# The second projection of a gated feed-forward layer as seven half-size products

## The chip, the cores and the metric

One of the cores of a Trainium2 chip runs the kernel. TensorE (PE) does the matrix products into PSUM, VectorE (DVE), ScalarE (ACT) and GpSimd (POOL) do the element-wise work, and SyncE (SP) issues all transfers between SBUF and DRAM. The metric is the time of one execution in device microseconds (us), the median of several runs.

## The reference, cut to what matters

One decoder layer on 16 learned tokens and 1024 tokens of width 1024: a mixer (a state-space group beside an attention group, then an output projection), and a feed-forward layer of width D_FF = 2816. The change is in the last two lines of the feed-forward layer:

```
gu = xn @ w_up                                   # first projection: 1024 -> 2 * 2816
g = causal_dwconv(gu[..., :D_FF], ffn_conv_w, ffn_conv_b)
f = (gelu(g) * gu[..., D_FF:]) @ w_down          # second projection: 2816 -> 1024
h = h + rms_norm(f, ffn_post_g)
return h[:, N_META:]
```

All data are float32. Each operand of a large product is split into a rounded part and the rest (hi and lo), and three of the four partial products are summed, so a block of 128 features costs three matmul instructions.

## The kernel before, in words

The first projection (class `Problem`, lines 963 to 1097) is already done in seven half-size products. A problem is one pair of 128-feature blocks of either the gate half (`g`, gu = 0) or the other half (`u`, gu = 1); there are 22 problems, g0, u0, g1, u1 to g10, u10. `product(n)` does one of the seven products (order 1, 6, 5, 7, 2, 3, 4) into PSUM banks called A, X and Y, and `post(n)` has DVE and ACT add the banks up. For g, `scale` (ACT) and `taps` (two DVE instructions) do the convolution and `gelu` (ACT) follows. For u, `after_u` multiplies the sums into the gate's tile `ga`, one tile of 128 features x 1024 tokens for each of the pair's two blocks. A finished tile is stored to DRAM (`fd[j]`, lines 1093 and 1097), 512 KB each.

While PE works at a problem, ACT and POOL make the next problem's weights: POOL forms sums of weight quarters (`sums`, lines 975 to 979) and the lo parts (line 958, 128x1024). The order on PE, DVE, ACT and POOL is the order in which the code is written, from the sixth token block of the output projection to `order.close()`; SP's order is a scheduler's.

The second projection (lines 1302 to 1343) walks the 22 feature blocks in eleven groups of two. For each block `down_operands` loads the activations `fr` and the weights `wr` (512 KB each) and splits them (ACT copies, POOL and DVE subtract). For each of 8 token blocks and 2 halves of the output columns, six matmuls of 512 columns go into a PSUM bank, which ACT (first group) or DVE adds to `facc` in SBUF. In the last group each token block is then normalised, added to the residual `ht` and stored to `out`.

Of the kernel before, what the change touches and what calls it, by code (L numbers as in the profile page):

```python
# [16 lines left out]
P = 128  # L17
# [31 lines left out]
def tile_layer(ctx: ExitStack, tc: tile.TileContext, x, meta, rows, parts,  # L49
# [913 lines left out]
    class Problem:  # L963
# [102 lines left out]
        def after_u(self, n, cs):  # L1066
            if n == 1:
                pu = f1.tile([P, 1032], F32, tag="fa", name=f"pu{self.p}")
                pv = f1.tile([P, 1032], F32, tag="fb", name=f"pv{self.p}")
                self.t = pu[:, 0:512], pu[:, 512:1024], pv[:, 0:512]  # L1070
            p1, u2, u3 = self.t
            A, X, Y = (self.acc[a][:, 0, :] if a in self.acc else None for a in "AXY")
            j1, j2 = 2 * self.p, 2 * self.p + 1
            add = nc.vector.tensor_tensor

            def times(j, half, src):
                d = acts[j][:, 512 * half:512 * half + 512]
# [163 lines left out]
    def down_operands(pool, j, fpool_, ftag, fbufs=1):  # L1241
        b = j % 2
        fr = fpool_.tile([P, T], F32, tag=ftag, name=f"fr{j}", bufs=fbufs)
        nc.sync.dma_start(out=fr, in_=fd[j])
        wr = wp.tile([P, D], F32, tag="wraw", name=f"wdr{j}")
        nc.sync.dma_start(out=wr, in_=w_down[j * P:(j + 1) * P, :])
        fh, fl, wh, wl = (pool.tile([P, T], F32R, tag=f"{n}{b}", name=f"{n}{j}") for n in ("fh", "fl", "wdh", "wdl"))
        nc.scalar.activation(wh, wr, AF.Copy)  # L1248
        nc.gpsimd.tensor_tensor(wl, wr, wh.bitcast(F32), op=ALU.subtract)  # L1249
        nc.scalar.activation(fh, fr, AF.Copy)  # L1250
        nc.vector.tensor_tensor(fl, fr, fh.bitcast(F32), op=ALU.subtract)  # L1251
        return fh, fl, wh, wl

    for i in range(1, NFF):
        q = probs[i]
# [6 lines left out]
        for m in (5, 6, 7, 3, 4) if i == 1 else (1, 6, 5, 7, 2, 3, 4):  # L1262
# [37 lines left out]
    fpool.close()  # L1300
    bpool.close()
    psum_stage("psE")


    db = down.enter_context(tc.tile_pool(name="db", bufs=1, side="left"))
    pools.append(db)
    facc = db.tile([P, NT, D], F32, name="facc", tag="facc")
    gfp = db.tile([P, D], F32, name="gfp", tag="gfp")
    nc.sync.dma_start(out=gfp, in_=rows[3:4, :].to_broadcast([P, D]))
    NG = NFF // 2  # L1310
    for grp in range(NG):
        cur = ops
        if grp + 1 < NG:
            ops = [down_operands(pools[(grp + 1) % 2], 2 * (grp + 1) + jj, db, "fr", 2) for jj in range(2)]
        for t in range(NT):
            for hf in range(2):
                acc = stage[0][1].tile([P, 512], F32, tag="dn", name=f"dn{grp}_{t}_{hf}", bufs=6)
                cs = slice(512 * hf, 512 * hf + 512)
                for kk, (fh, fl, wh, wl) in enumerate(cur):
                    for i, (u, v) in enumerate(((fh, wh), (fl, wh), (fh, wl))):  # L1320
                        mm(acc, u[:, t * P:(t + 1) * P], v[:, cs], start=(kk == 0 and i == 0),  # L1321
                           stop=(kk == 1 and i == 2))
                dst = facc[:, t, cs]
                if grp == 0:
                    nc.scalar.activation(dst, acc, AF.Copy)
                else:
                    nc.vector.tensor_tensor(dst, acc, dst, op=ALU.add)  # L1327
            if grp < NG - 1:
                continue
            ht = wp.tile([P, D], F32, tag="wraw", name=f"ht{t}")  # L1330
            nc.sync.dma_start(out=ht, in_=h1d[t])
            ft = facc[:, t, :]
            junk = db.tile([P, D], F32, tag="fr", name=f"ftmp{t}", bufs=2)
            ss = db.tile([P, 1], F32, tag="fss", name=f"fss{t}", bufs=2)
            nc.scalar.activation(junk, ft, AF.Square, accum_out=ss)
            r = rstd_of(db, ss, 1, P, f"fo{t}")
            fg = db.tile([P, D], F32, tag="fg", name=f"fg{t}", bufs=2)
            nc.vector.tensor_tensor(fg, ft, gfp, op=ALU.mult)  # L1338
            nc.vector.scalar_tensor_tensor(fg, fg, r, ht, op0=ALU.mult, op1=ALU.add)  # L1339
            nc.sync.dma_start(out=out[t * P:(t + 1) * P, :], in_=fg)  # L1340
# [56 lines left out]
```

## Time and profile before

| | us |
|---|---|
| median of 3 runs | 1934.86 (1933.71 to 1937.4) |
| the profiled execution | 1934.62 |
| its span, first to last instruction | 1932.9 |
| TensorE busy | 1804.6 (93%) |
| VectorE busy | 1042.8 (54%) |
| ScalarE busy | 720.1 (37%) |
| GpSimd busy | 925.6 (48%) |
| first matmul of the second projection starts at | 1675.22 |
| last matmul of the second projection starts at | 1917.18 |

The span counts from the first instruction of the program to the last; 1.7 us of the time lie outside it. Matmuls are pipelined: one of 512 columns is shown as 0.39 us long, but the next one starts earlier than that, so the pace is read from start to start.

### The profile page before, as it was taken

The page shows a single profiled execution, that of the slowest core. Times are in us where ns is not written, and L with a number is a line of the kernel's source. Part 1 is how long each engine was busy: PE and PEld are TensorE (multiplying, and loading weights), DVE is VectorE, ACT ScalarE, POOL GpSimd, SP SyncE. Part 2 cuts the span into 40 slices and gives each one's busy share as a digit, 9 for nine tenths or more (in the row PEclk, how much of TensorE's full clock was granted, in tenths as well). Part 3 has the DMA queues.
Part 4 walks back from the last instruction along what each step waited for, and adds up shares of the span by engine and source line. Part 5 has one row for each costly group of instructions (what it writes and reads, how often), then busy time and mean ns, then how long its engine had stood idle before and what let it go on. Part 6 is the DMA issues. An engine that isn't in the chain of part 4 may idle for free. (4 is left out here: it accounts for less than half of the span.)

```text
span 1932.9 us, 27268 instructions
## 1 busy us (share of the span) xinstructions
PE 1804.6 (93%) x11053; PEld 1535.2 (79%) x11053; DVE 1042.8 (54%) x1179; ACT 720.1 (37%) x1158; POOL 925.6 (48%) x651
## 2 busy tenths in 40 slices
PE   6899999999899999999799999799999999999996
PEld 5899889887677877877477677688999889788885
DVE  5552963674555454545632256755445554456777
ACT  5423552534444444434533333433333333421211
POOL 2223653665555455444343133667776777322320
PEclk9999999999999999999999999899999999999998
DMA  4133333220101101100322554122322222332234
GB/s 146 44 86 104 98 115 106 61 83 33 34 23 34 34 23 34 34 23 12 101 82 72 170 181 141 61 88 70 106 67 87 66 80 95 123 107 88 97 100 152
DMA packets 72721, 157.43 MB, mean 81 GB/s; under 512 B 9642, under 2 KB 34634, under 8 KB 72596
## 3 DMA queue, kind: packets, MB, share of 16 engines
q1 hardware_dynamic: 72596, 155.69, 25.5%
q8 instruction: 87, 1.43, 0.3%
q14 instruction: 38, 0.31, 0.1%
HBM read 114.53 MB, written 41.14 MB: 81 GB/s over the span
## 5 line engine op out<-in xcount | busy, mean ns | idle before, releaser
L581 POOL TENSOR_TENSOR bt<-bt,kp 128x256 f32<-128x256 f32 (+7 forms) x128 | 212.7, 1681 | 236.0 <-DVE kp L579 229.7
L579 DVE TENSOR_TENSOR_SCAN kp<-kp,hold 128x272 f32<-128x272 f32 (+7 forms) x128 | 175.5, 1409 | 182.6 <-ACT kp L575 109.6
L1327 DVE TENSOR_TENSOR facc<-dn,facc 128x512 f32<-128x512 f32 x160 | 106.8, 686 | 66.4 <-PE dn L1321 66.2
L1321 PE MATMUL dn<-wdh,fh 128*128 128x512 f32 x352 | 138.3, 393 | 2.9 <-DVE pu L1095 2.9
L1249 POOL TENSOR_TENSOR wdl<-wdr,wdh 128x1024 fp32r<-128x1024 f32 x22 | 61.7, 2826 | 165.1 <-ACT wdh L1248 165.1
L1321 PE MATMUL dn<-wdh,fl 128*128 128x512 f32 x352 | 138.0, 392 | 0.0
L1321 PE MATMUL dn<-wdl,fh 128*128 128x512 f32 x352 | 137.9, 392 | 0.0
L958 POOL TENSOR_TENSOR wl<-wr,wh 128x1024 fp32r<-128x1024 f32 x46 | 115.8, 2527 | 34.4 <-ACT wh L957 31.4
L595 PE MATMUL tw<-ident,bt 128*128 128x128 f32 x576 | 81.9, 280 | 21.4 <-issue 13.8
L616 PE MATMUL av<-th,v 128*64 128x128 f32 x1152 | 80.3, 280 | 19.6 <-DVE th L602 19.4
L575 ACT ACTIVATE kp<-z 128x288 f32<-128x288 f32 (+6 forms) x112 | 82.8, 739 | 36.4 <-PE z L574 36.1
L595 PEld LDWEIGHTS tw<-ident,bt 128*128 128x128 f32 x576 | 63.1, 142 | 41.6 <-issue 27.4
L616 PEld LDWEIGHTS av<-th,v 128*64 128x64 f32 x1152 | 62.5, 137 | 39.9 <-DVE th L602 26.8
L957 ACT ACTIVATE wh<-wr 128x1024 fp32r<-128x1024 f32 x46 | 48.6, 1058 | 119.3 <-PE fX L1015 74.1
L574 PE MATMUL z<-k,q 64*128 64x144 f32 (+6 forms) x448 | 87.0, 489 | 3.2 <-ACT bt L576 3.2
L1059 DVE SCALAR_TENSOR_TENSOR ga<-gr,pp,ga 128x1024 f32<-128x1024 f32 x44 | 70.6, 1604 | 30.5 <-ACT ga L1052 29.8
L576 ACT ACTIVATE bt<-z 128x288 f32<-128x288 f32 (+6 forms) x112 | 83.1, 742 | 0.0
L1248 ACT ACTIVATE wdh<-wdr 128x1024 fp32r<-128x1024 f32 x22 | 23.0, 1052 | 155.8 <-PE dn L1321 142.3
L1321 PEld LDWEIGHTS dn<-wdh,fh 128*128 128x128 f32 x352 | 66.8, 190 | 17.2 <-issue 3.3
L1321 PEld LDWEIGHTS dn<-wdh,fl 128*128 128x128 f32 x352 | 66.8, 190 | 14.0
L1321 PEld LDWEIGHTS dn<-wdl,fh 128*128 128x128 f32 x352 | 66.7, 190 | 13.9
L1103 POOL TENSOR_TENSOR al<-wr,ah 128x512 fp32r<-128x512 f32 x21 | 32.0, 1525 | 81.9 <-ACT ah L1102 81.9
(429 smaller groups left out, 5691.3 us busy)
## 6 DMA issues: line engine op xcount, KB each, us to landing
wr<-in_w_up SPq DMA_DIRECT2D x45, 512.0 KB, 3.6
fd<-ga SPq DMA_DIRECT2D x22, 512.0 KB, 4.5
wdr<-in_w_down SPq DMA_DIRECT2D x22, 512.0 KB, 4.4
fr<-fd SPq DMA_DIRECT2D x22, 512.0 KB, 4.6
yk<-yd SPq DMA_DIRECT2D x16, 512.0 KB, 3.9
zd<-zt SPq DMA_DIRECT2D x8, 520.0 KB, 3.3
xt<-in_x SPq DMA_DIRECT2D x8, 512.0 KB, 8.9
wr_X<-in_w_xbc SPq DMA_DIRECT2D x8, 512.0 KB, 3.8
```

The source lines that it names most:

```text
L574: mm(z[:, j, :w], q[h, t0:t0 + P], k[h, a:a + w], start=True, stop=True)
L575: nc.scalar.activation(kp[:, :, a:a + w], z[:, :, :w], AF.Sigmoid, scale=-QSCALE)
L576: nc.scalar.activation(bt[:, :, a:a + w], z[:, :, :w], AF.Sigmoid, scale=QSCALE)
L579: nc.vector.tensor_tensor_scan(kp[:, j][:, ::-1], kp[:, j][:, ::-1], hold[:, L - n:L][:, ::-1], 1.0, op0=ALU.mult, op1=ALU.max)
L581: nc.gpsimd.tensor_tensor(bt[:, j, 0:m], bt[:, j, 0:m], kp[:, j, 1:m + 1], op=ALU.mult)
L595: nc.tensor.transpose(tw[:, j, b, :], bt[:, j, c0:c0 + P], ident)
L616: mm(av[halves[j], :], v[:, kb, halves[j]], th[:, j, b, :], start=kb == 0, stop=kb == i)
L958: nc.gpsimd.tensor_tensor(l, raw, h.bitcast(F32), op=ALU.subtract)
L1059: nc.vector.scalar_tensor_tensor(v, self.g[jj][:, :, i:i + 256], fconv_w[:, j, i:i + 1], v, op0=ALU.mult, op1=ALU.add)
L1249: nc.gpsimd.tensor_tensor(wl, wr, wh.bitcast(F32), op=ALU.subtract)
L1321: mm(acc, u[:, t * P:(t + 1) * P], v[:, cs], start=(kk == 0 and i == 0), stop=(kk == 1 and i == 2))
L1327: nc.vector.tensor_tensor(dst, acc, dst, op=ALU.add)
```

## The change

The second projection becomes seven half-size products as well. Activations and weights of a pair of blocks are cut in quarters: features of the first or second block, first or second 512 tokens (or output columns). Each product is summed over all eleven pairs in PSUM, in 77 steps of 12 matmuls, before it is read: `DOWN` names the products in their order. The sums of activation quarters (`s1` to `s4`) are made by DVE in the first projection, in the next pair's g problem (`f_sums`), and kept in DRAM beside the quarters `a11`, `a12`, `a22`; sums of weight quarters are made by DVE in place (`w_sum`), in weights that are loaded once and stay in SBUF. All lo parts are made by DVE; POOL has nothing left there but the inverse roots. Each step fetches one 256 KB activation quarter four steps ahead and splits both operands three steps ahead, into three rotating pairs of tiles. The first four token blocks are finished while products 7 and 4 run, the other four at the end.

```diff
+DOWN = [(1, "a11", "b11"), (2, "a12", "b21"), (3, "s4", "b22"), (6, "s2", "t2"), (5, "s1", "b11"), (7, "s3", "b12"),
+        (4, "a22", "b21")]
...
-    fd = [dr.tile([P, T], F32, name=f"fd{j}", tag=f"fd{j}") for j in range(NFF)]
+    fd = [{n: dr.tile([P, 512], F32, name=f"fd{n}{p}", tag=f"fd{n}{p}")
+           for n in ("a11", "a12", "a22", "s1", "s2", "s3", "s4")} for p in range(NPR)]
...
+        def f_sums(self, part):
+            (a11, a21), (a12, a22) = ((f[:, :512], f[:, 512:]) for f in self.f)
+            sub = nc.vector.tensor_tensor
+            if part:
+                sub(a12, a12, a11, op=ALU.subtract)
+                self.store("s4", a12)
+                return
+            sub(a22, a21, a22, op=ALU.add)
+            sub(a21, a11, a21, op=ALU.subtract)
+            sub(a11, a22, a11, op=ALU.subtract)
+            for n, a in (("s1", a22), ("s3", a21), ("s2", a11)):
+                self.store(n, a)
...
+    def split_step(s):
+        n, a, b, p = steps2[s]
+        hi = wp.tile([P, 2, 512], F32R, tag="whi", name=f"dh{s}", bufs=WB)
+        lo = wp.tile([P, 2, 512], F32R, tag="wlo", name=f"dl{s}", bufs=WB)
+        sub = nc.vector.tensor_tensor
+        if n == 6:
+            wd["t2", p] = db.tile([P, 512], F32, tag="t2", name=f"t2_{p}", bufs=2)
+            sub(wd["t2", p], wd["b22", p], wd["b11", p], op=ALU.subtract)
+        for k, raw in enumerate((araw.pop(s), wd[b, p])):
+            nc.scalar.activation(hi[:, k], raw, AF.Copy)
+            sub(lo[:, k], raw, hi[:, k].bitcast(F32), op=ALU.subtract)
+        dops[s] = hi, lo
...
                 if m == 7:
                     tB.close()
...
+                    for k in range(8):
+                        fetch_w(da, ("b11",), k)
+                        if k < 4:
+                            fetch_a(k)
+                    split_step(0)
+                elif m in (2, 3):
+                    split_step(m - 1)
                 continue
+            if i > 1 and q.gu == 0 and m in (7, 4):
+                probs[i - 1].f_sums(m == 4)
...
+            for i, (u, v) in enumerate(((hi, hi), (lo, hi), (hi, lo))):
+                mm(banks[t], u[:, 0, c], v[:, 1, :], start=(p == 0 and i == 0), stop=(p == NPR - 1 and i == 2))
...
+    for k in range(3):
+        down_mm(k, (3,))
+    for k in range(3):
+        down_mm(k, (0, 1, 2))
+    for s in range(n2):
+        n, a, b, p = steps2[s]
+        if s > 2 and s < n2 - 3:
+            down_mm(s, (3, 0, 1, 2))
+        elif s == n2 - 3:
+            for act in todo:
+                act()
+            for t in range(4):
+                for k in range(3):
+                    down_mm(s + k, (t,))
+                evac2(n, t, banks[t])
+                half_tail(1, t, 0)
+                close_tail(1, t, 0)
+                if t > 0:
+                    end_tail(1, t - 1)
+            end_tail(1, 3)
+            break
...
+        if s + 4 < n2:
+            fetch_a(s + 4)
+        if s + 3 < n2:
+            split_step(s + 3)
+        for args in W_SUMS.get(s, ()):
+            w_sum(*args)
+        if todo:
+            todo.pop(0)()
```

Not shown: the stores of `a11`, `a12` and `a22` in `after_u` right behind the products that finish them, the loads, the table `W_SUMS` (one weight sum a step in steps 15 to 40 and 48 to 51, two in steps 41 to 47) and `evac2`, which adds the finished banks to `facc`, one bank in each of the steps after a product's end.

The order on VectorE in problem g5, from product 6 to the first sum of u5. Names: `gr` are g5's sums, `fX`, `fY`, `fA` PSUM banks, `ga10` and `ga11` the pair's tiles, `pu`, `pv` sums of u. Before:

```order
L1041 TENSOR_TENSOR gr5_1_12113<-fY05_12151,gr5_1_12113 128x516
L1043 TENSOR_TENSOR gr5_0_12114<-fY05_12151,gr5_0_12114 128x516
L1059 SCALAR_TENSOR_TENSOR ga10_12264<-gr5_0_12114,pp_90,ga10_12264 128x1024 x2
L1045 TENSOR_TENSOR gr5_1_12113<-fX05_12120,gr5_1_12113 128x516
L1059 SCALAR_TENSOR_TENSOR ga11_12293<-gr5_1_12113,pp_90,ga11_12293 128x1024 x2
L1083 TENSOR_TENSOR pu5_12315<-fX15_12323,pu5_12315 128x512
```

And now:

```order
L1045 TENSOR_TENSOR gr5_1_12205<-fY05_12243,gr5_1_12205 128x516
L1115 TENSOR_TENSOR ga9_12043<-ga8_12012,ga9_12043 128x512
L1116 TENSOR_TENSOR ga8_12012<-ga8_12012 128x512
L1117 TENSOR_TENSOR ga8_12012<-ga9_12043,ga8_12012 128x512
L1047 TENSOR_TENSOR gr5_0_12206<-fY05_12243,gr5_0_12206 128x516
L1063 SCALAR_TENSOR_TENSOR ga10_12362<-gr5_0_12206,pp_90,ga10_12362 128x1024 x2
L1049 TENSOR_TENSOR gr5_1_12205<-fX05_12212,gr5_1_12205 128x516
L1112 TENSOR_TENSOR ga9_12043<-ga9_12043,ga8_12012 128x512
L1063 SCALAR_TENSOR_TENSOR ga11_12393<-gr5_1_12205,pp_90,ga11_12393 128x1024 x2
L1087 TENSOR_TENSOR pu5_12415<-fX15_12423,pu5_12415 128x512
```

Three additions on the tiles of the pair before (`ga8`, `ga9`) now stand between the additions of products 7 and 3, and one between product 4's and the taps of `ga11`.

The order on VectorE in the last problem u10, from product 7 on. Names: `ga20`, `ga21` the last pair's tiles, `fl` lo parts of activations before, `dl` lo parts of a step's operands now, `ar` a fetched activation quarter, `b11` a weight quarter. Before:

```order
L1078 TENSOR_TENSOR ga21_13994<-pv10_14013,ga21_13994 128x512
L1251 TENSOR_TENSOR fl0_14067<-fr0_14062,fh0_14066 128x1024
L1251 TENSOR_TENSOR fl1_14079<-fr1_14074,fh1_14078 128x1024
L1078 TENSOR_TENSOR ga20_13965<-fA110_13999,ga20_13965 128x512
L1091 TENSOR_TENSOR pu10_14012<-fY110_14030,pu10_14012 128x512
L1078 TENSOR_TENSOR ga20_13965<-pu10_14012,ga20_13965 128x512
L1095 TENSOR_TENSOR pu10_14012<-fX110_14016,pu10_14012 128x512
```

And now:

```order
L1082 TENSOR_TENSOR ga21_14139<-pv10_14158,ga21_14139 128x512
L1289 TENSOR_TENSOR dl0_14233<-ar0_14210,dh0_14232 128x512
L1289 TENSOR_TENSOR dl0_14233<-b11_0_14208,dh0_14232 128x512
L1082 TENSOR_TENSOR ga20_14108<-fA110_14144,ga20_14108 128x512
L1289 TENSOR_TENSOR dl1_14253<-ar1_14214,dh1_14252 128x512
L1289 TENSOR_TENSOR dl1_14253<-b11_1_14212,dh1_14252 128x512
L1097 TENSOR_TENSOR pu10_14157<-fY110_14175,pu10_14157 128x512
L1082 TENSOR_TENSOR ga20_14108<-pu10_14157,ga20_14108 128x512
L1289 TENSOR_TENSOR dl2_14273<-ar2_14218,dh2_14272 128x512
L1289 TENSOR_TENSOR dl2_14273<-b11_2_14216,dh2_14272 128x512
L1100 TENSOR_TENSOR pu10_14157<-fX110_14161,pu10_14157 128x512
```

The two long subtractions have become six half as long, spread between the additions of products 7, 2, 3 and 4. On TensorE the first nine matmuls of the second projection now go to a bank that is not one of X or Y (`dn1_3`, three for each of the steps 0 to 2).

## Rows read from the trace of the kernel before

**Rows 1.** Stretches: us, busy time (x instructions) by engine, granted clock, DMA share, GB/s.

```profile
1270.00:1675.00 405.00, 402.30 (x2534) 361.71 (x2533) 204.33 (x185) 135.06 (x151) 281.38 (x157) 1.00 0.26 81
1675.00:1918.00 243.00, 242.35 (x1056) 200.16 (x1056) 159.75 (x193) 54.69 (x68) 59.28 (x25) 0.99 0.33 111
```

**Rows 2.** Timeline, TensorE, second projection: start, us, engine, line, what, [idle before].

```profile
1675.22 0.77 PE L1321 MATMUL dn<-wdh,fh 128*128 128x512 f32 x1 [2.92 <-DVE pu L1095]
...
1681.21 0.40 PE L1321 MATMUL dn<-wdl,fh 128*128 128x512 f32 x1
...
1917.18 0.39 PE L1321 MATMUL dn<-wdl,fh 128*128 128x512 f32 x1
```

**Rows 3.** A stretch as in Rows 1, at the second projection's start.

```profile
1675.20:1680.80 5.60, 5.58 (x13) 4.49 (x14) 0.60 (x1) 2.12 (x3) 0.99 (x1) 0.50 0.62 244
```

**Rows 4.** Timeline, VectorE and GpSimd, last problem u10.

```profile
1667.99 4.56 DVE L1251 TENSOR_TENSOR fl<-fr,fh 128x1024 fp32r<-128x1024 f32 x2
1673.78 0.69 DVE L1078 TENSOR_TENSOR ga<-pu,ga 128x512 f32<-128x512 f32 x1
1674.39 0.68 DVE L1095 TENSOR_TENSOR pu<-fX,pu 128x512 f32<-128x512 f32 x1
...
1665.11 5.22 POOL L1249 TENSOR_TENSOR wdl<-wdr,wdh 128x1024 fp32r<-128x1024 f32 x2 [11.82 <-ACT wdh L1248]
```

**Rows 5.** Timeline, VectorE, last part of g5 and start of u5.

```profile
1445.58 0.70 DVE L1041 TENSOR_TENSOR gr<-fY,gr 128x516 f32<-128x516 f32 x1
1450.61 0.70 DVE L1043 TENSOR_TENSOR gr<-fY,gr 128x516 f32<-128x516 f32 x1 [4.33 <-PE fY L1015]
1452.81 3.71 DVE L1059 SCALAR_TENSOR_TENSOR ga<-gr,pp,ga 128x1024 f32<-128x1024 f32 x2 [1.50 <-ACT ga L1052]
1456.44 0.69 DVE L1045 TENSOR_TENSOR gr<-fX,gr 128x516 f32<-128x516 f32 x1
1458.44 2.60 DVE L1059 SCALAR_TENSOR_TENSOR ga<-gr,pp,ga 128x1024 f32<-128x1024 f32 x2 [1.31 <-ACT ga L1052]
1460.96 0.68 DVE L1083 TENSOR_TENSOR pu<-fX,pu 128x512 f32<-128x512 f32 x1
```

**Rows 6.** Timeline, GpSimd, the same stretch.

```profile
1445.96 2.39 POOL L958 TENSOR_TENSOR wl<-wr,wh 128x1024 fp32r<-128x1024 f32 x1 [1.83 <-ACT wh L957]
1449.36 2.41 POOL L958 TENSOR_TENSOR wl<-wr,wh 128x1024 fp32r<-128x1024 f32 x1 [1.01 <-ACT wh L957]
1451.72 2.40 POOL L958 TENSOR_TENSOR wl<-s,wh 128x1024 fp32r<-128x1024 f32 x1
```

**Rows 7.** Timeline, GpSimd and VectorE, later in u5.

```profile
1467.53 5.22 POOL L958 TENSOR_TENSOR wl<-wr,wh 128x1024 fp32r<-128x1024 f32 x2
1472.72 2.85 POOL L958 TENSOR_TENSOR wl<-s,wh 128x1024 fp32r<-128x1024 f32 x1
...
1471.09 2.21 DVE L1078 TENSOR_TENSOR ga<-pu,ga 128x512 f32<-128x512 f32 x1
1473.94 2.18 DVE L1078 TENSOR_TENSOR ga<-pu,ga 128x512 f32<-128x512 f32 x1
```

**Rows 8.** Timeline, TensorE, u5, from product 5 to product 7.

```profile
1461.18 0.40 PE L1015 MATMUL fY<-t1l,wh 128*128 128x512 f32 x1
1461.41 0.39 PE L1015 MATMUL fY<-t1h,wl 128*128 128x512 f32 x1
1461.70 0.50 PE L1015 MATMUL fX<-t3h,wh 128*128 128x512 f32 x1
```

**Rows 9.** Timeline, ScalarE, a copy of 128x512.

```profile
1459.26 0.58 ACT L1081 ACTIVATE pu<-fA 128x512 f32<-128x512 f32 x1
```

**Rows 10.** Transfers by line: what, queue, count, KB each, us to landing.

```profile
xk<-xsd SPq DMA_DIRECT2D x16, 256.0 KB, 2.9
```

**Rows 11.** Timeline, VectorE, the last token blocks.

```profile
1917.08 1.29 DVE L1339 SCALAR_TENSOR_TENSOR fg<-fg,rs_fo,ht 128x1024 f32<-128x1024 f32 x1
...
1927.91 1.28 DVE L1339 SCALAR_TENSOR_TENSOR fg<-fg,rs_fo,ht 128x1024 f32<-128x1024 f32 x1 [0.73 <-POOL rs_fo L188]
```

More of the change, by code (lines that the diff above doesn't have):

```diff
@@ L1239, in tile_layer @@
     down = ExitStack()
[L1241 to L1252, printed above, removed]
+    steps2 = [(n, a, b, p) for n, a, b in DOWN for p in range(NPR)]
@@ new lines, in tile_layer, with fetch_w, fetch_a @@
+    wd, dops, araw = {}, {}, {}
+    def fetch_w(pool, names, p):
+        for nm in names:
+            jj, hf = int(nm[1]) - 1, int(nm[2]) - 1
+            wd[nm, p] = pool.tile([P, 512], F32, tag=f"{nm}{p}", name=f"{nm}_{p}")
+            r0 = (2 * p + jj) * P
+            nc.sync.dma_start(out=wd[nm, p], in_=w_down[r0:r0 + P, 512 * hf:512 * hf + 512])
+    def fetch_a(s):
+        n, a, b, p = steps2[s]
+        pool, tag = (da, "ar") if s % 2 else (wp, "wraw")
+        araw[s] = pool.tile([P, 512], F32, tag=tag, name=f"ar{s}", bufs=2)
+        nc.sync.dma_start(out=araw[s], in_=fd[p][a])
@@ L1297, in tile_layer @@
                 q.taps(1)
-    order.close()
[L1300 to L1340, printed above, removed]
@@ new lines, in tile_layer, with down_mm @@
+    stage[0][0].close()
+    pse = down.enter_context(tc.tile_pool(name="psE", bufs=1, space=PSUM))
+    banks = {}
+    def down_mm(s, tbs):
+        n, a, b, p = steps2[s]
+        hi, lo = dops[s]
+        for t in tbs:
+            if p == 0:
+                banks[t] = psum_mm(f"dn{n}_{t}") if t == 3 else pse.tile([P, 512], F32, tag="dn", name=f"dn{n}_{t}",
+                                                                        bufs=6)
+            c = slice(t * P, (t + 1) * P)
+            for i, (u, v) in enumerate(((hi, hi), (lo, hi), (hi, lo))):
+                mm(banks[t], u[:, 0, c], v[:, 1, :], start=(p == 0 and i == 0), stop=(p == NPR - 1 and i == 2))
@@ new lines, in evac2 @@
+    def evac2(n, t, acc):
+        add = nc.vector.tensor_tensor
+        if n == 1:
+            nc.scalar.activation(facc[1, 0, t], acc, AF.Copy)
+        elif n == 2:
+            add(facc[0, 0, t], acc, facc[1, 0, t], op=ALU.add)
+        elif n == 3:
+            nc.scalar.activation(facc[0, 1, t], acc, AF.Copy)
+        elif n == 6 or n == 4:
+            add(facc[1, 0, t], acc, facc[1, 0, t], op=ALU.add)
+        elif n == 5:
+            add(facc[0, 1, t], acc, facc[0, 1, t], op=ALU.add)
+            add(facc[1, 1, t], acc, facc[1, 0, t], op=ALU.add)
+        elif n == 7:
+            add(facc[1, 0, t], acc, facc[1, 0, t], op=ALU.add)
+            add(facc[1, 1, t], acc, facc[1, 1, t], op=ALU.add)
@@ new lines, in tile_layer, with open_tail, half_tail @@
+    slots = [ta.tile([P, 4 * HW], F32, tag=f"{n}{e}", name=f"slot{n}{e}") for n in ("b22", "t4") for e in "hl"]
+    tails = {}
+    def open_tail(h, t):
+        tb_ = 4 * h + t
+        fg = slots[t][:, 0:D]
+        ht = slots[t][:, D:2 * D]
+        nc.sync.dma_start(out=ht, in_=h1d[tb_])
+        ms = db.tile([P, 4], F32, tag="fms", name=f"fms{tb_}", bufs=4)
+        tails[h, t] = fg, ht, ms
+    def half_tail(h, t, hf):
+        fg, ht, ms = tails[h, t]
+        f = facc[h, hf, t]
+        c = slice(512 * hf, 512 * hf + 512)
+        junk = db.tile([P, 512], F32, tag="t2", name=f"jt{h}{t}{hf}", bufs=2)
+        nc.scalar.activation(junk, f, AF.Square, accum_out=ms[:, hf:hf + 1])
+        nc.vector.tensor_tensor(fg[:, c], f, gfp[:, c], op=ALU.mult)
@@ new lines, in scale_tail, with close_tail, end_tail @@
+    def scale_tail(h, t, last):
+        fg, ht, ms = tails[h, t]
+        first = 1 - last
+        nc.vector.tensor_scalar(ms[:, 2:3], ms[:, first:first + 1], 1.0 / D, EPS, op0=ALU.mult, op1=ALU.add)
+    def close_tail(h, t, last):
+        fg, ht, ms = tails[h, t]
+        nc.vector.tensor_scalar(ms[:, 3:4], ms[:, last:last + 1], 1.0 / D, ms[:, 2:3], op0=ALU.mult, op1=ALU.add)
+        nc.gpsimd.tensor_tensor(ms[:, 3:4], ms[:, 3:4], nhalf[:, 0:1], op=ALU.pow)
+    def end_tail(h, t):
+        fg, ht, ms = tails.pop((h, t))
+        nc.vector.scalar_tensor_tensor(fg, fg, ms[:, 3:4], ht, op0=ALU.mult, op1=ALU.add)
+        r0 = (4 * h + t) * P
+        nc.sync.dma_start(out=out[r0:r0 + P, :], in_=fg)
```

68 lines of the change are left out of this document (62 added, 6 removed).

## The prediction

> **What bounds the kernel now.** I read the stretches first, since one share for the whole span hides the stages. In the first projection (1270 to 1675 us) TensorE is busy 402.3 of 405.0 us, in the second 242.35 of 243.0 [rows 1]; VectorE has 204 and 160 us there and GpSimd 281 and 59. So TensorE sets the end of both stages, and a gain must come from fewer matmuls, from its waits, or from what follows its last matmul. Next I read TensorE's timeline. Of the 1056 matmuls of the second projection the first starts at 1675.22, after 2.92 us of waiting for VectorE, the fifteenth at 1681.21 and the last at 1917.18 [rows 2]. From the fifteenth on the pace is (1917.18 - 1681.21) / 1041 = 0.2267 us. The first 14 intervals took 5.99 us instead of 14 x 0.2267 = 3.17: in that stretch the granted clock is 0.50, that is 1.2 GHz, against 2.4 GHz later [rows 3]; what went ahead of it is the idle stretch of 2.92 us. The third thing is the end: TensorE is done at 1917.18 + 0.39 = 1917.57, the span ends at 1932.9, 15.3 us later.
>
> **Matmuls removed.** Seven products x 11 pairs x 12 matmuls = 924 against 1056, of the same shape (128x128 weights, 512 columns). 132 x 0.2267 = **-29.9 us**. This counts only if operands are ready for 77 steps of 12 x 0.2267 = 2.72 us each.
>
> *Feeding a step.* The operand tiles of a step are three steps old, so its split can begin when TensorE ends step s and must be ready two steps later, 5.44 us. It takes two ScalarE copies (0.58 us each [rows 9]) and VectorE's last subtraction (0.69 us, the row of 1673.78 [rows 4], with GpSimd silent): 1.9 us, so 3.5 us are spare. VectorE's own load is two subtractions a step, up to five operations of 0.69 us = 3.45 us in steps 44 to 47 (two lo parts, two weight sums, one bank): 0.73 us too much in each of four steps, 2.9 us behind, inside the 3.5. Over the stage it has 154 lo parts, 55 weight sums, 32 bank and sum additions, 16 multiplications and 3 sums at the start, 260 x 0.69 = 179 us, and 8 final ones of 1.28 us: 190 of 209 us. So I take the feeding at 0; without that cover each 0.1 us that a step is late would cost 77 x 0.1 = 7.7 us. GpSimd's 62 us of lo parts end, so VectorE meets nobody there.
>
> *Transfers.* 77 activation quarters and 44 weight quarters of 256 KB are loaded, and residual, output, gain row and four sums moved: 41.7 MB in 209 us = 200 GB/s. The kernel before moved 111 GB/s in this stage on average, but 244 GB/s at a DMA share of 0.62 in its first 5.6 us [rows 1, 3], so the rate exists. A quarter is fetched when the tile four steps back is split, which leaves about 4 x 2.72 - 1.9 = 9 us; a 256 KB load lands in 2.9 us [rows 10]. I take 0.
>
> **The start.** Before, VectorE was late because two 128x1024 subtractions that were queued ahead of its PSUM additions took 4.56 us, from 1667.99 on; GpSimd's two lo parts ran from 1665.11 to 1670.33 beside them, and the addition at 1674.39 freed the bank that the first matmul waited for [rows 4]. Now six half-size subtractions stand between the additions, GpSimd does none of them, and the first nine matmuls (9 x 0.2267 = 2.0 us) go to another bank. Weight quarters can be loaded only when product 7 ends (about 1663.9, three products of 12 x 0.23 us ahead of the second projection): +0.3 us issue, +2.9 landing, +1.9 splitting = 1669, three us ahead of TensorE's arrival at 1672.3; the splits of steps 1 and 2 follow products 2 and 3 by about 2.5 us and are in time by about half a us. I take the whole wait and the slow clock behind it away: 2.92 + (5.99 - 3.17) = **-5.7 us**; the other end is 0, if the loads land some 3 us later.
>
> **The end.** The last three steps are walked by token block, 9 matmuls (2.04 us) each. A block then costs VectorE one bank addition (0.68 us), one half-width multiplication (0.69), a short scalar step (0.15) and the previous block's final operation (1.28 [rows 11]): about 2.7 us, so it falls behind by 0.7 us a block, three times. Behind the last matmul: 0.1 + 2.1 lag, 0.68 + 0.69 + 0.15, two final operations 2.6: 6.3 us; before, the last final operation ended at 1927.91 + 1.28 = 1929.19 and the span 3.7 us later, for the last store. 10.0 or, with short overlaps of VectorE's instructions, 9.7 us instead of 15.3: **-5.6 us** (bounds -3, if ScalarE's squares come in between, and -7).
>
> **The first projection.** Here the change adds VectorE work: four additions of 128x512 with both operands in SBUF per pair, for ten pairs (the eleventh's fall into the second projection), and five more stores, each behind work that is done. The loads of w_up that queue behind these on SP are wanted a problem later, so I put them at 0.
>
> VectorE is not free here. After its g additions end at 1446.28 it idles 4.33 us until product 3 [rows 5]; then follow the addition of product 3 (line 1043), ScalarE's scaling, two taps (line 1059), the addition of product 4 (line 1045), scaling and taps of the second block, and u's first sum (line 1083), which ends at 1461.64. TensorE starts product 7 at 1461.70, 0.29 us behind the matmul ahead of it, against a pace of about 0.23: it waits for this sum already [rows 8]. So whatever delays that chain is paid by TensorE.
>
> The added operations collide with GpSimd. In [rows 7] an addition from SBUF started at 1471.09 and took 2.21 us instead of 0.69: GpSimd's instruction ended at 1472.75 (1467.53 + 5.22), VectorE's 0.55 us after that; the next GpSimd instruction took 2.85 instead of 2.40 us. So each waits until the other's running instruction is over, and they take turns. The three additions at 1446.28 meet GpSimd's lo part of 1445.96 to 1448.35, then its idle 1.01 us, then two more without a gap until 1454.12 [rows 6]. Three additions need 3 x 0.55 = 1.65 us of GpSimd's absence and find 1.01, so GpSimd's last instruction ends 0.64 us later. The taps of 1452.81 could not run before that end already (they ended at 1456.52, 2.4 us behind it), so they and the whole chain move by 0.64 us. The fourth addition falls into the 1.31 us in which VectorE waits for ScalarE [rows 5], with GpSimd idle. Ten pairs x 0.64 = **+6.4 us**. Bounds: 0, if the gap grows, and 27 us, if GpSimd keeps its turn: then the third addition waits for 1454.12, the addition of product 3 ends 4.2 us late and the taps, behind 1.24 us of ScalarE and 2.4 of their own, 2.7 us late in each pair. I take the turns, as in rows 7.
>
> **The sum**, against the profiled execution's 1934.6 (its span and 1.7 us around it; the median is 1934.9, so they may be taken as one): 1934.6 - 29.9 - 5.7 - 5.6 + 6.4 = **1899.8 us**.
>
> **Rivals.**
> 1. *The additions are free in the first projection*: 1893.4. For it speaks 4.33 us of idle time, against it rows 7. The Trainium skill, "SBUF", section "Who interferes with whom", says that a VectorE instruction with two SBUF inputs and a GpSimd instruction that reads SBUF lock each other out for a whole instruction; by that rule, the trace agrees (2.21 against 0.69 us), this rival needs a longer gap.
> 2. *GpSimd keeps its turn*: 1899.8 + 20.6 = 1920.
> 3. *The start waits as before*, because the loads come late: 1899.8 + 5.7 = 1905.5.
> 4. *Loads are the bound, slower than before*: were the 121 loads of 256 KB served one behind the other at 2.9 us [rows 10], they would take 351 us against 209, and the time would be 1899.8 + 142 = 2042. It decides from the point where the 41.7 MB move at under 171 GB/s (in 209 + 35 = 244 us). Against it: 244 GB/s in rows 3, and nothing forces one at a time. Beside this stands a rule against small transfers: the Trainium skill, "DMA: Bandwidth & Descriptors", section "Bandwidth", wants 1 MiB or more per transfer for three quarters of the peak; rows 3, with 512 KB transfers, show 244 GB/s, and no row here shows the rate of a stream of 256 KB.
> 5. *Fewer matmuls do not bring their share*, because three per bank in place of six, or a short wait per step, lengthen the step by 0.05 us: 77 x 0.05 = +4: 1904.
>
> **Chances.** Forecast (within about 5 us of 1900) 0.55; rival 1 0.17; rival 2 0.08; rival 3 0.10; rival 4 0.05; rival 5 0.05. The range 1890 to 1914 holds the forecast, rivals 1, 3 and 5 with their spreads and leaves out 2 and 4, and some of the tails: about 0.8. Faster by over 0.2% (about what a measurement of this kernel can tell from no change) 0.94, within it 0.01, slower 0.05, all of it rival 4.
>
> **What would show it.** 924 matmuls at 0.227 us, their first within 0.1 us of the first projection's last, at a granted clock of 1.0; the stage from there to the end of the span about 219 us (260.6 before, from 1672.3 on). The first projection's ten later pairs longer by about 0.6 us each, with TensorE waiting at product 7 of u for line 1087; if that wait is absent rival 1 holds, if it is 2.7 us rival 2. Waits of TensorE on ScalarE copies or loads inside the second projection would make the feeding wrong. VectorE's last operation about 6 us behind the last matmul.

## The result

The kernel after takes 1902.8 us (median of 4 runs, 1902.23 to 1903.68) against 1936.11 us before on the same chip (4 runs, 1933.71 to 1937.4): a ratio of 0.983, 95% interval 0.9813 to 0.9847. It is faster by 1.7%. The forecast was 1899.8 us in a range of 1890 to 1914. The profiled execution took 1902.23 us, span 1900.4, against 1934.62 and 1932.9; the terms below are compared between these two.

**TensorE's two stages.** Stretches of the kernel after (columns as in [rows 1]), the first from 1270 us to the end of the first projection, the second over the second projection:

```profile
1270.00:1679.80 409.80, 403.47 (x2537) 362.04 (x2536) 253.43 (x227) 135.78 (x153) 283.13 (x156) 1.00 0.31 97
1679.80:1890.00 210.20, 210.09 (x925) 173.15 (x923) 167.69 (x276) 98.29 (x185) 5.57 (x6) 1.00 0.56 181
```

TensorE is still the bound of both. The second projection now takes 210 us where [rows 1] had 243 and ahead of that 2.9 of waiting; the first projection takes more. One of the three groups of matmuls from the list of the costliest groups (three times 308 = 924), and TensorE's timeline at both ends of the second projection:

```profile
L1367 PE MATMUL dn<-dl,dh 128*128 128x512 f32 x308 | 119.9, 389 | 0.1
```

```profile
1679.60 0.39 PE L1019 MATMUL fX<-t4h,al 128*128 128x512 f32 x1
1679.83 0.40 PE L1367 MATMUL dn<-dh 128*128 128x512 f32 x1
...
1882.52 0.50 PE L1367 MATMUL dn<-dh 128*128 128x512 f32 x1
1882.86 0.39 PE L1367 MATMUL dn<-dh,dl 128*128 128x512 f32 x1
1883.33 0.50 PE L1367 MATMUL dn<-dl,dh 128*128 128x512 f32 x1
...
1889.59 0.39 PE L1367 MATMUL dn<-dl,dh 128*128 128x512 f32 x1
```

From the last matmul of the first projection to the first of the second it is 0.23 us, one ordinary pace: the wait of [rows 2] is gone, and with it the stretch at a granted clock of 0.50 of [rows 3]. The last matmul ends at 1889.98. From the first to the last start there are 923 intervals in 209.76 us; 0.51 us of that are four longer intervals from 1882.3 to 1883.7 (the first of the four token blocks of the walk reaches step 76 before its operands are split); the other intervals are 0.2267 us each.

**TensorE's waits** from 1270 us on (us in total, times, longest):

```profile
PE fX L1019 <- DVE pu L1087: 5.1, 10, 0.5
PE fA L1019 <- POOL wl L962: 1.2, 1, 1.2
```

The second comes once, at the start of g1, and takes back what TensorE had lost less ahead of it: from the first matmul of the first projection to the start of g1 it is 69.8 us, against 71.1 before. The first is the wait that was forecast: ten pairs, product 7 of u. In the timeline of u5 it is the row

```profile
1466.24 0.50 PE L1019 MATMUL fX<-t3h,wh 128*128 128x512 f32 x1 [0.51 <-DVE pu L1087]
```

and the matmul ahead of it started 0.9 us earlier, against 0.29 in [rows 8]. So each pair pays about 0.6 us. From start to start, u1 to u9 take 20.27 to 20.30 us each, where the kernel before took 19.62 to 19.70, and g2 to g10 20.17 as against 20.18; u10 shows the same wait.

**Term by term**, us:

| | forecast | measured | where it is read |
|---|---|---|---|
| 132 matmuls less | -29.9 | -29.9 | 924 at 0.2267 |
| feeding a step | 0 | +0.5 | four intervals near 1883 |
| transfers | 0 | 0 | TensorE never waits behind one |
| start of the second projection | -5.7 | -5.9 | no wait, clock 1.00; from start to start |
| end | -5.6 | -4.9 | 15.3 to 10.45 behind the last matmul |
| additions in the first projection | +6.4 | +6.4 | ten u problems, 0.64 each |
| start of the first projection | not named | +1.2 | 1203.92 against 1202.71 |
| sum | -34.8 | -32.4 (0.2 unassigned) | |

The term that was not named lies ahead of all that the change touches: the first matmul of the first projection starts 1.2 us later. Over the nine experiments below, which leave that part as it is in the kernel after, the same matmul starts between 1202.1 and 1206.1, on both sides of the kernel before. So it is scatter of single executions, and the reason why stages are compared below wherever one run must do.

### The profile page after: what moved, and what is told of

It reads as the page before. It is cut to its first block, busy times and chain, and to the rows that moved or that the text cites. A ratio compares the mean times of both kernels' runs of the same rounds, so it can differ in the third digit from the quotient of the medians.

```text
span 1900.4 us, 27411 instructions
## 1 busy us (share of the span) xinstructions
PE 1773.1 (93%) x10921; PEld 1509.2 (79%) x10921; DVE 1095.8 (58%) x1298; ACT 762.5 (40%) x1276; POOL 873.2 (46%) x629
## 5 line engine op out<-in xcount | busy, mean ns | idle before, releaser
L1367 PE MATMUL dn<-dl,dh 128*128 128x512 f32 x308 | 119.9, 389 | 0.1
L1367 PE MATMUL dn<-dh 128*128 128x512 f32 x308 | 119.9, 389 | 0.0
L1367 PE MATMUL dn<-dh,dl 128*128 128x512 f32 x308 | 119.8, 389 | 0.0
L1413 POOL TENSOR_TENSOR fms<-fms,nhalf 128x1 f32<-128x1 f32 x8 | 8.5, 1060 | 225.8 <-DVE fms L1412 225.8
L1288 ACT ACTIVATE dh<-ar 128x512 fp32r<-128x512 f32 x77 | 48.7, 632 | 111.6 <-PE dn L1367 88.2
L1289 DVE TENSOR_TENSOR dl<-ar,dh 128x512 fp32r<-128x512 f32 x77 | 53.2, 690 | 42.2 <-ACT dh L1288 42.2
L1063 DVE SCALAR_TENSOR_TENSOR ga<-gr,pp,ga 128x1024 f32<-128x1024 f32 x44 | 59.9, 1361 | 23.0 <-ACT ga L1056 22.2
L1367 PEld LDWEIGHTS dn<-dh 128*128 128x128 f32 x308 | 57.8, 188 | 12.4 <-ACT dh L1288 0.3
L1367 PEld LDWEIGHTS dn<-dl,dh 128*128 128x128 f32 x308 | 57.8, 188 | 12.3 <-DVE dl L1289 0.4
L1367 PEld LDWEIGHTS dn<-dh,dl 128*128 128x128 f32 x308 | 57.8, 188 | 12.0
```

What stands on the lines that cost most here:

```text
L1063: nc.vector.scalar_tensor_tensor(v, self.g[jj][:, :, i:i + 256], fconv_w[:, j, i:i + 1], v, op0=ALU.mult, op1=ALU.add)
L1289: sub(lo[:, k], raw, hi[:, k].bitcast(F32), op=ALU.subtract)
L1367: mm(banks[t], u[:, 0, c], v[:, 1, :], start=(p == 0 and i == 0), stop=(p == NPR - 1 and i == 2))
```

## Experiments

All start from the kernel after; line numbers are those of its profile. Those with an interval were timed against the kernel before on the same chip (medians there 1933.08, 1934.34 and 1935.54 us in the three groups e1 to e3, e6 and e7, and e9).

### Is it the three sums, and is it SBUF?

e1 leaves the three additions out in the ten g problems, the calls that pass `q` (the eleventh pair's, in the second projection, stay):

```diff
-        def f_sums(self, part):
+        def f_sums(self, part, x=None):
...
-            sub(a22, a21, a22, op=ALU.add)
-            sub(a21, a11, a21, op=ALU.subtract)
-            sub(a11, a22, a11, op=ALU.subtract)
+            if x is None:
+                sub(a22, a21, a22, op=ALU.add)
+                sub(a21, a11, a21, op=ALU.subtract)
+                sub(a11, a22, a11, op=ALU.subtract)
...
-                probs[i - 1].f_sums(m == 4)
+                probs[i - 1].f_sums(m == 4, q)
```

> The three additions behind product 7 are left out in the ten g problems (their stores stay, so s1, s2 and s3 of ten pairs are not the sums). Theory (these additions delay the chain that ends in u's first sum by 0.62 us a pair): the wait of TensorE at product 7 of u goes, ten problems shorten by 0.6 us, 1902.8 - 6.3 = 1896.5 us. Rival (the five extra stores or the fourth addition cause the wait): no change, 1902.8.

e2 has, behind the lines of e1, three additions of the same size in the same place, with one operand from a PSUM bank (`X`) in place of SBUF (their results are not the sums):

```diff
+            else:
+                ps_ = x.acc["X"][:, :, :256]
+                for a in (a22, a21, a11):
+                    v = a.rearrange("p (c n) -> p c n", n=256)
+                    sub(v, ps_, v, op=ALU.add)
```

> The three additions stay where they are, with as many elements, but take one operand from a PSUM bank instead of SBUF (so s1, s2 and s3 of ten pairs are not the sums). Theory (turns with GpSimd at SBUF cost the time): each takes 0.69 us also beside GpSimd, the wait goes, 1896.5 us. Rival (VectorE's time as such is too much there): three times 0.69 us stand in the chain as before, the wait of 0.6 us a pair stays, 1902.8 us.

Measured: e1 1896.44 us, 0.981 (0.9791 to 0.983); e2 1897.28 us, 0.9813 (0.9797 to 0.9829). The intervals overlap that of the kernel after, so the stages decide: in both the u problems u1 to u10 are back at 19.66 to 19.71 us (one of 19.94 in e2). The fourth addition and the five stores stay in e1, so they cost nothing. VectorE and GpSimd in g5 of the kernel after:

```profile
1450.14 2.70 DVE L1115 TENSOR_TENSOR ga<-ga,ga 128x512 f32<-128x512 f32 x1
1452.88 0.69 DVE L1116 TENSOR_TENSOR ga<-ga 128x512 f32<-128x512 f32 x1
1453.61 2.78 DVE L1117 TENSOR_TENSOR ga<-ga,ga 128x512 f32<-128x512 f32 x1
1456.32 0.68 DVE L1047 TENSOR_TENSOR gr<-fY,gr 128x516 f32<-128x516 f32 x1
1458.36 2.70 DVE L1063 SCALAR_TENSOR_TENSOR ga<-gr,pp,ga 128x1024 f32<-128x1024 f32 x2 [1.36 <-ACT ga L1056]
...
1449.91 2.39 POOL L962 TENSOR_TENSOR wl<-wr,wh 128x1024 fp32r<-128x1024 f32 x1 [1.90 <-ACT wh L961]
1453.30 2.54 POOL L962 TENSOR_TENSOR wl<-wr,wh 128x1024 fp32r<-128x1024 f32 x1 [1.00 <-ACT wh L961]
1455.79 2.87 POOL L962 TENSOR_TENSOR wl<-s,wh 128x1024 fp32r<-128x1024 f32 x1
```

and the same place in e2 (VectorE, then GpSimd):

```profile
1451.33 1.88 DVE L1123 TENSOR_TENSOR ga<-fX,ga 128x512 f32<-128x512 f32 x3
...
1451.09 2.40 POOL L962 TENSOR_TENSOR wl<-wr,wh 128x1024 fp32r<-128x1024 f32 x1 [1.90 <-ACT wh L961]
1454.48 2.42 POOL L962 TENSOR_TENSOR wl<-wr,wh 128x1024 fp32r<-128x1024 f32 x1 [0.99 <-ACT wh L961]
1456.86 2.39 POOL L962 TENSOR_TENSOR wl<-s,wh 128x1024 fp32r<-128x1024 f32 x1
```

With both operands in SBUF the first sum ends at 1452.84, 0.54 us behind the end of GpSimd's instruction (1452.30); the second falls for the most part into GpSimd's idle time; the third again ends 0.55 us behind an instruction of GpSimd (1455.84 to 1456.39), and GpSimd's next one takes 2.87 instead of 2.39 us. The two taps behind them end 2.40 us behind that instruction of GpSimd (1458.66 and 1461.06), as they did before (1454.12 and 1456.52 in [rows 5, 6]): the chain moves with the end of GpSimd's work. With one operand from PSUM the three additions run through in 1.88 us while GpSimd's instruction runs, and GpSimd's stays at 2.40. So it is the turns at SBUF that cost the 0.6 us, not VectorE's time. The Trainium skill, "SBUF", section "Who interferes with whom", says that a VectorE instruction with two SBUF inputs contends with a GpSimd instruction that reads SBUF. The trace agrees, with 2.70 and 2.78 against 0.69 us.

### The sums one product earlier

e3 changes one number: the sums go ahead of the additions of product 7, where GpSimd works at its weight sums of half that length.

```diff
-            if i > 1 and q.gu == 0 and m in (7, 4):
+            if i > 1 and q.gu == 0 and m in (5, 4):
```

> All is computed; the three additions stand ahead of product 7's additions instead of behind them, in 5.0 us in which VectorE waits for TensorE and in front of 1.9 us in which GpSimd waits for ScalarE. Theory (the turns cost only what the gaps don't hold): GpSimd's four sums end 1.65 us later, inside its 1.9 us, product 7's additions start on time, the wait goes, 1896.5 us. Rival (turns cost the same wherever they stand): GpSimd's three lo parts shift by up to 1.65 us and the wait stays, 1902 to 1904 us.

Measured: 1895.98 us (1895.08 to 1897.28), 0.9806 (0.9791 to 0.982); against 0.983 that is 4.6 us less, and u1 to u9 are back at 19.66 to 19.71 us (one of 19.94). TensorE's waits on line 1087 from 1315 us on, and the first rows of VectorE's timeline behind 1449 us in g5:

```profile
PE fX L1019 <- DVE pu L1087: 0.2, 1, 0.2
```

```profile
1452.99 0.70 DVE L1047 TENSOR_TENSOR gr<-fY,gr 128x516 f32<-128x516 f32 x1 [4.29 <-PE fY L1019]
1455.18 3.75 DVE L1063 SCALAR_TENSOR_TENSOR ga<-gr,pp,ga 128x1024 f32<-128x1024 f32 x2 [1.49 <-ACT ga L1056]
```

The 4.29 us of idle time ahead of product 3's addition are back and stay empty: the work has moved to idle time in which a turn is short. GpSimd's last weight sums beside them take 1.62 to 1.74 instead of 1.28 us, and nothing waits for them. The wait of 0.2 us that is left is the 19.94; apart from it the term of 6.4 us is recovered.

### The start of the second projection

e5 makes the splits of steps 0 to 2 behind product 4, in a row, in place of behind products 7, 2 and 3:

```diff
-                    split_step(0)
-                elif m in (2, 3):
-                    split_step(m - 1)
+                elif m == 4:
+                    for k in range(3):
+                        split_step(k)
```

> The splits of steps 0 to 2 stand behind product 4 of u10 and its additions instead of between the additions of products 7, 2 and 3. Theory (the start gained because VectorE has these lo parts ready): TensorE waits some 3.4 us in pieces over the first nine matmuls; if its clock falls to 1.2 GHz behind that as it did before, another 2.5 us: 1906 to 1909 us. Rival (the start gained by the other PSUM bank alone): at most 0.5 us more, 1903 us.

e8 leaves the splits and takes the banks of steps 0 to 2 in ordinary order:

```diff
-        down_mm(k, (3,))
-    for k in range(3):
-        down_mm(k, (0, 1, 2))
+        down_mm(k, (0, 1, 2, 3))
```

> The steps 0 to 2 take the banks in the order 0, 1, 2, 3 in place of bank 3 of all three steps ahead of the others, so that the first matmul of the second projection goes to a bank that VectorE's last addition of u10 has to free first. Nothing is left out. Theory (the start was won by the other bank as much as by the half-size splits): the addition that frees the bank ends about 1.5 us behind the end of the first projection, so TensorE waits about 1.5 us, and if the granted clock falls to 0.50 behind it, some 1.5 to 3 us more: 1904 to 1907. Rival (the half-size splits alone make the addition early enough): no wait, 1902 to 1903.

Measured (one run each): e5 1904.53 us, e8 1906.29 us. TensorE's timeline in e5 and a stretch behind its wait:

```profile
1677.91 0.40 PE L1367 MATMUL dn<-dh 128*128 128x512 f32 x1
1680.19 0.50 PE L1367 MATMUL dn<-dh,dl 128*128 128x512 f32 x1 [1.88 <-DVE dl L1289]
1680.79 0.59 PE L1367 MATMUL dn<-dl,dh 128*128 128x512 f32 x1
```

```profile
1681.20:1684.20 3.00, 3.00 (x8) 2.01 (x7) 1.94 (x4) 0.00 (x0) 0.00 (x0) 0.50 1.06 370
```

and in e8:

```profile
1683.81 0.47 PE L1367 MATMUL dn<-dh 128*128 128x512 f32 x1 [1.53 <-DVE pu L1100]
```

```profile
1683.80:1690.00 6.20, 6.19 (x27) 5.14 (x28) 1.88 (x3) 1.16 (x2) 0.00 (x0) 1.00 1.00 335
```

In e5 TensorE idles 1.88 us, then runs at a granted clock of 0.50 (1.2 GHz): with both, the second projection's start loses 4.2 us. That is less than the 3.4 us of waiting and 2.5 of slow clock expected, and the total lies under the expected range; the rival, 0.5 us at most, falls. That the total is only 2.3 us above the kernel after comes from the first projection, which ended 1.9 us earlier in this execution. In e8 the wait is 1.53 us and the clock stays at 1.00 behind it; the first matmul of the second projection starts 1.92 us behind the last of the first instead of 0.23, so the bank order alone is worth 1.7 us here (the other 2.3 us of its total lie ahead of it, 2.2 of them at the start of the first projection, 1206.11; without them the total would stand at 1904.0, where the expected range begins, since the slow clock held possible there did not come). So both halves of the new start are needed: the splits spread between VectorE's additions, and the bank that nothing has to free. The slow clock comes with the idle time, as the start's term had it: 0.50 behind 2.92 us in the kernel before and behind 1.88 in e5, where only the splits have moved, and 1.00 behind 1.53 in e8 and in the kernel after, one execution each.

### How far feeding is from the bound

e6 gives VectorE two more subtractions in each of the steps 6 to 32:

```diff
+        for k in range(2 if 5 < s < 33 else 0):
+            xj = db.tile([P, 512], F32, tag="xj", name=f"xj{s}{k}")
+            nc.vector.tensor_tensor(xj, wd["b11", 0], wd["b11", 1], op=ALU.subtract)
```

> Two more subtractions of 128x512, on weights in SBUF, are given to VectorE in each of the steps 6 to 32 (54 in all, about 33 to 37 us of VectorE's time). Theory (feeding has a cover of about 3.3 us a step; VectorE then needs about 3.05 us in each of the steps 15 to 32 against TensorE's 2.72 us, and falls behind by 18 x 0.33 = 5.9 us, of which the cover takes 3.3): about 2.5 us longer, 1904 to 1907; at 0.69 us for each of VectorE's instructions, up to 9.7 us longer. Rival (feeding is at its limit, every instruction of VectorE is paid by TensorE): 54 x 0.61 = 33 us longer, 1935.

e7 adds 20 loads of 256 KB:

```diff
+        if 5 < s < 26:
+            xj = slots[s % 4][:, 512 * (s // 4 % 2):512 * (s // 4 % 2) + 512]
+            nc.sync.dma_start(out=xj, in_=w_down[s % NFF * P:s % NFF * P + P, 512:])
```

> One more load of 256 KB from DRAM in each of the steps 6 to 25 (5.2 MB in all, into free tiles that nobody reads), while the DMA share is at 0.95 or above already. Theory (the loads run about 9 us ahead of their need and ahead of a stage in which the DMA engines are idle again, so what is late there eats spare time only): the crowded stretch grows by about 5.2 MB at 334 GB/s = 15 us, the landings grow from about 5 to 6 or 7 us, TensorE waits for little, 0 to 4 us longer, 1902 to 1907. Rival (the transfers were the bound of that stretch): each added load is paid in full, 20 x 0.26 MB at 334 GB/s = 16 us longer, 1918.

Measured: e6 1910.97 us, 0.9883 (0.9867 to 0.99), that is 0.53% or 10 us above the kernel after; e7 1900.65 us, 0.9829 (0.9815 to 0.9844), no change.

In e6 the waits of TensorE in the second projection, a stretch, and two rows of VectorE a step apart are:

```profile
PE dn L1367 <- ACT dh L1288: 2.5, 4, 0.7
PE dn L1367 <- DVE dl L1289: 1.0, 3, 0.3
```

```profile
1748.00:1770.00 22.00, 20.36 (x79) 13.98 (x77) 21.79 (x37) 6.40 (x11) 0.00 (x0) 1.00 0.23 72
```

```profile
1741.87 0.68 DVE L1289 TENSOR_TENSOR dl<-ar,dh 128x512 fp32r<-128x512 f32 x1
...
1745.01 0.69 DVE L1289 TENSOR_TENSOR dl<-ar,dh 128x512 fp32r<-128x512 f32 x1
```

VectorE is full there (21.79 of 22 us). A step with five operations takes 3.14 us of it. From start to start the intervals of TensorE above 0.2267 us add up to 9.5 us more than in the kernel after, all in steps 26 to 36. The expectation of 2.5 us was too low by my count of operations: it left out four bank additions (steps 22 to 25) and three sums `t2` (steps 30 to 32). With them: 18 x (3.14 - 2.72) + 4 x 0.6 + 3 x 0.78 = 12.3 us behind, less the cover of 3.3 us = 9.0. So the cover is there, as large as the timeline of the kernel after shows it (in most steps the last lo part ends 3.2 to 3.3 us ahead of the step's first matmul, in steps 48 to 54, behind the densest ones, at least 2.1, and in steps 3 to 6, behind the start, 1.4 to 2.9), and what goes beyond it is paid in full. The rival, every instruction paid, would have been 33 us.

For e7, stretches of the kernel after (the last two columns are the DMA share and GB/s):

```profile
1690.00:1700.00 10.00, 10.00 (x45) 8.26 (x45) 6.66 (x12) 4.72 (x9) 0.00 (x0) 1.00 0.99 345
1700.00:1740.00 40.00, 40.00 (x178) 33.12 (x177) 22.76 (x36) 18.46 (x34) 0.00 (x0) 1.00 0.95 334
1740.00:1750.00 10.00, 10.00 (x46) 8.29 (x45) 8.18 (x14) 4.50 (x8) 0.00 (x0) 1.00 0.52 163
1750.00:1890.00 140.00, 139.90 (x616) 115.04 (x614) 124.04 (x207) 67.49 (x131) 5.57 (x6) 1.00 0.39 117
```

and of e7, with ScalarE's waits for the quarters that it splits:

```profile
1700.00:1740.00 40.00, 40.00 (x178) 33.14 (x177) 22.82 (x36) 19.27 (x34) 0.00 (x0) 1.00 1.01 359
1740.00:1750.00 10.00, 10.00 (x46) 8.29 (x45) 8.51 (x15) 4.35 (x8) 0.00 (x0) 1.00 0.91 330
```

```profile
ACT dh L1288 <- DMA ar<-fda: 5.7, 4, 2.0
```

The added loads make the crowded stretch longer, ScalarE waits 5.7 us in place of 2.8 for quarters, and TensorE waits for none of it. The landings grew less than expected (median of the weight quarters 5.4 us against 5.2). The transfers use nearly all of the DMA engines' time for 60 us and are still not the bound, since they run ahead of their need.

### The end

e4 runs the last three steps in ordinary order and the four blocks behind them:

```diff
-        if s > 2 and s < n2 - 3:
+        if s > 2:
...
-        elif s == n2 - 3:
+        if s == n2 - 1:
...
-                for k in range(3):
-                    down_mm(s + k, (t,))
```

> The last three steps are no longer walked by token block: they run in the ordinary order, step by step over the four banks, and the four last token blocks are finished behind them. Nothing is left out. Theory (the walk by block lets VectorE work on three of the four blocks while TensorE still runs): VectorE's four blocks of about 2.85 us can begin only 1.4 us ahead of the last matmul, when the first of the banks is complete, in place of about 5.5 us ahead, so the stretch behind the last matmul grows from 10.5 to about 14.5 us (3.5 to 5 more) and the time is near 1906 to 1908. Rival (the stretch behind the last matmul is set by the last block's own chain alone): no change, 1902 to 1903.

e9 starts from e3 and goes the other way: the last four steps are walked by token block (not shown: the operands of the very last step are split two steps earlier, into tiles of dead weights).

```diff
-        elif s == n2 - 3:
+        elif s == n2 - 4:
...
-                for k in range(3):
+                for k in range(4):
```

> Built on the version with the early sums (median 1895.98 us): the last four steps are walked by token block in place of three, so a block is 12 matmuls (2.72 us) and VectorE's 2.85 us for a block nearly keep up; the operands of the very last step are split early into tiles of weights that nobody reads any more. Nothing is left out. Theory (10.5 us behind the last matmul hold 1.9 us of VectorE's lag, gathered by 2.85 us against 2.04 us a block): the lag falls to 0.1 + 2 x 0.13 = 0.4 us, the stretch behind the last matmul to about 9.0 us, and the time is 1894.0 to 1895.0. Rival (the stretch is the last block's own chain and the store): unchanged, 1896; or the earlier split delays the steps in front, 1896 to 1898.

Measured: e4 1906.89 us (one run), with 14.59 us behind the last matmul; e9 1895.01 us (1894.22 to 1897.86), 0.9792 (0.9779 to 0.9805), with 8.77 us. The kernel after has 10.45. VectorE and SyncE at the end of the kernel after (the last block's addition, its final operation, the last store):

```profile
1891.89 0.68 DVE L1378 TENSOR_TENSOR facc<-dn,facc 128x512 f32<-128x512 f32 x1
...
1895.27 1.29 DVE L1417 SCALAR_TENSOR_TENSOR slott4l<-slott4l,fms 128x1024 f32<-128x1024 f32 x1 [0.44 <-POOL fms L1413]
...
1896.59 0.33 SPq L1419 DMA_DIRECT2D out<-slott4l  x1
```

the first block's addition in e4 (its last matmul ends at 1890.53):

```profile
1889.20 0.69 DVE L1378 TENSOR_TENSOR facc<-dn,facc 128x512 f32<-128x512 f32 x1 [3.51 <-PE dn L1367]
```

and the last block's in e9 (its last matmul ends at 1883.87):

```profile
1884.10 0.69 DVE L1382 TENSOR_TENSOR facc<-dn,facc 128x512 f32<-128x512 f32 x1
```

In the kernel after, VectorE comes to the last block 1.91 us behind the last matmul; in e4 it begins the first of the four only 1.3 us ahead of it, and the stretch is 4.1 us longer (the walk's wait of 0.5 us goes in return; the rest of the difference in total lies ahead of the second projection); in e9 its lag is 0.23 us and the stretch 1.7 us shorter. Of that, 0.5 us go back: from the first to the last matmul of the second projection it is 210.23 instead of 209.76 us, for the most part because the walk, which begins a step earlier, waits 0.86 instead of 0.51 us for operands. Against e3 the median is 1.0 us lower and the ratio 0.0014, with intervals that overlap, so only the stages show the gain. The interval of e9 lies clear below that of the kernel after; that of e3 overlaps it by a little (0.982 against 0.9813), and there the u problems show the gain.

## Why the prediction held, and where it was off

**Matmuls** and **start**: right in mechanism, and nearly in size. The pace stayed at 0.2267 us with three matmuls per bank (rival 5 falls), and the loads were in time (rival 3 falls). The last matmul of the first projection in the kernel before,

```profile
1671.91 0.39 PE L1015 MATMUL fX<-t4h,al 128*128 128x512 f32 x1
```

starts 3.31 us ahead of the second projection's first [rows 2], and now it is 0.23: 3.1 us less, where the prediction took the 2.92 us of idle time, which count from that matmul's shown end. So the term is 5.9 us. The margin that the start rests on was given as half a microsecond for step 2; on VectorE's timeline in u10

```profile
1680.10 0.69 DVE L1289 TENSOR_TENSOR dl<-b,dh 128x512 fp32r<-128x512 f32 x1
1680.70 0.69 DVE L1100 TENSOR_TENSOR pu<-fX,pu 128x512 f32<-128x512 f32 x1
```

step 2's last lo part ends at 1680.79, 0.4 us ahead of its first matmul (1681.19), and the addition of line 1100 at 1681.39, 0.5 us ahead of the matmul that needs its bank (1681.87).

**Additions in the first projection**: right. 0.64 us for a pair by counting turns in [rows 5 to 7], 0.64 measured, and e2 shows the cause. Rival 1 (idle time makes them free) and rival 2 (GpSimd keeps its turn) both fall: the third sum ended behind GpSimd's second instruction, not its third.

**Feeding**: no wait in 76 of 77 steps. VectorE's load was put too high, 190 us against 167.69 in the stretch above and 173.5 to the end of the span, since each instruction was counted at its duration (0.69 us); in a row, instructions start every 0.60 us, as in 1680.10 and 1680.70. So the densest steps took 1.1 us of the cover (3.28 down to 2.14) where 2.9 were forecast. The one step at fault, 76, was not looked at by itself: it is split when step 73 ends, as every step, but the walk by token block wants it 6 matmuls later instead of 24. That is the +0.5.

**Transfers**: the sum came out right, the picture behind it did not. I took 200 GB/s on average over the stage and compared it with 244 GB/s of [rows 3]. The average hides that the loads bunch: 345 and 334 GB/s at a DMA share of 0.99 and 0.95 from 1690 to 1740, then 163 and 117. The page's list of transfers (KB each, median us to landing):

```profile
b<-in_w_down SPq DMA_DIRECT2D x44, 256.0 KB, 5.2
ar<-fds SPq DMA_DIRECT2D x44, 256.0 KB, 2.7
ar<-fda SPq DMA_DIRECT2D x33, 256.0 KB, 4.4
```

against 2.9 in [rows 10]. Rival 4 needed under 171 GB/s and fell by a factor of two. The Trainium skill, "DMA: Bandwidth & Descriptors", section "Bandwidth", asks for 1 MiB or more per transfer for three quarters of the peak. The trace shows no such limit at 256 KB: many in flight together moved 334 GB/s at a share of 0.95, and 359 at 1.01 in e7.

**End**: the mechanism was right (VectorE falls behind block by block), its count was not. The additions of the first three blocks,

```profile
1884.52 0.68 DVE L1378 TENSOR_TENSOR facc<-dn,facc 128x512 f32<-128x512 f32 x1
...
1886.18 0.68 DVE L1378 TENSOR_TENSOR facc<-dn,facc 128x512 f32<-128x512 f32 x1
...
1889.04 0.68 DVE L1378 TENSOR_TENSOR facc<-dn,facc 128x512 f32<-128x512 f32 x1
```

and the last at 1891.89 lie 1.66, 2.86 and 2.85 us apart: the first block has no final operation of a block ahead of it, so VectorE loses time twice, not three times, but 0.8 us each time and not 0.7. That the lag came out near, 1.91 us against 2.2, is in part luck. The size of the chain behind it was short: 4.67 us from the last block's addition to the end of its final operation, against 4.1. The missing half microsecond is two small waits of the last block: 0.13 us for ScalarE's square ahead of the scalar step, and the 0.44 us for GpSimd in the row of 1895.27. From there to the end of the span it is 3.87 us against 3.7.

## What to carry to other kernels

Count the turns, not the idle time, when VectorE work with both operands in SBUF is put beside GpSimd: 1.9 us of additions in 4.3 us of idle time still cost 0.64 us in each of ten pairs, and moved ahead by one product, or with one operand read from PSUM, they cost next to nothing. When a projection ends in a chain on another engine, choose how many steps are walked block by block so that a block's matmuls last as long as that chain's work on a block (2.04, 2.72 and 2.85 us here). An average rate over a stage says neither that transfers have room nor that they are the bound; how far they run ahead of their need does.

## What was not expected of the hardware

Behind 1.53 us without a matmul the granted clock stayed at 1.00 (e8), behind 1.88 us it was 0.50 (e5, the 3.0 us stretch shown, with matmuls every 0.43 us), and behind 2.92 us in the kernel before it was 0.50 for the 5.6 us of [rows 3]; ten waits of 0.5 us, 40 us apart, left it at 1.00. Each of these is one run. And the DMA engines moved 370 GB/s in the 3 us stretch of e5 shown above, at a share that the profile gives as 1.06, half as much again as the 244 GB/s of [rows 3], where the share was 0.62. The kernel before shows such a rate too, behind that stretch: from 1681.2 to 1684.2 it moved 363 GB/s at a share of 1.00, so the prediction could have read it there.
